# RMSNorm and a projection by 15 products: three transposes moved to TensorE, loads merged, the order laid out anew

## Chip, core and metric

The kernel runs on one core of a Trainium2 chip. The metric is the device time of one execution in microseconds. Engines: TensorE (PE; PEld is its weight load), VectorE (DVE), ScalarE (ACT), GpSimd (POOL), SyncE (SP), which here only issues DMA transfers, and 16 DMA engines behind its queue.

## The reference

```python
batch, n_heads, seq, head_dim = 8, 12, 1024, 64     # x is 8 x 1024 x 768, w_qkv is 768 x 2304
rms = np.sqrt(np.mean(x ** 2, axis=-1, keepdims=True) + eps)
x_norm = x / rms * gamma
return np.matmul(x_norm, w_qkv).astype(np.float32)
```

Inputs and output are float32. There are 8192 rows of x, 64 tiles of 128 rows; the output is 75.5 MB.

## The kernel before

**Two kinds of tiles.** The first seven tiles of x (the head, `N_HEAD`) are multiplied in the plain way. A tile is loaded (`load_x`), cast to bf16 (`cast`), turned by six 128x128 transposes on TensorE (`tr`, L509) and copied out of PSUM (`cp`); then six matmuls of 384 columns (`mm`, L520) give each of six column blocks, which are scaled by 1/rms on the way out of PSUM (`evac`) and stored (`store_h`). `stat` and `recip` give 1/rms: a square with a running sum on ScalarE, a root, a reciprocal. The weights come in twelve pieces of 576 KB (`load_w`) and are multiplied by gamma and cast to bf16 (`conv`). Gamma is turned from a row into columns by one transpose on TensorE (`gamma_tr`) and copied out by VectorE (`gamma_cp`). Fourteen matmuls on zeros (`idle`, L481) fill TensorE at the start.

**Triples.** The other 57 tiles are taken in 19 triples. Of a triple, three row blocks by two halves of K give six blocks of A; a half of the columns (1152) gives, by two halves of K and three column blocks, six blocks of B. The 18 block products of such a piece are computed as 15, of sums and differences of blocks. The sums of B are made once (`bound`, `scales`, `quad`, `bsum`, in f16 with one scale per half). For each triple:

- `load_t` (L580) loads a tile of x, one issue per tile, 384 KB; a triple's buffer `XI` is one of three.
- `pstat` (L583) squares it on ScalarE with a running sum, `prms` and `precip` give 1/rms for three tiles.
- `pcast` (L450 on ScalarE, L455 on VectorE) scales it to f16 into one of two buffers `XB`.
- `pxbar` (L602) turns the triple by one DMA transpose from SBUF to SBUF into one of three buffers `XT`. The functions `ptr` and `pcp`, six transposes on TensorE for a tile and a copy out of PSUM, are there and are not called by the order before.
- `osum` (L460) makes the eleven sums of A, mostly on GpSimd.
- `product` (L624) is three matmuls of 128x384. The 15 products of a triple and column half run in two chains (`CHAIN`), each in one PSUM bank, and add on to what the chain has; after each product the bank is read before the next product of the chain goes on.
- `hold` (L450 on ScalarE) reads a bank, scaled, into a part of the output the first time; `join` (L636, VectorE) reads it and adds or subtracts a part held before.
- `pstore` (L640) stores 128 rows by 1152 columns, 576 KB.

**What sets the order.** Everything is emitted in one order written out as text (`PLAN`): each item has a name, the engine and its arguments, and the loop at the end calls the function of that name. Each engine works through its own items in that order; between engines, waits are put in where data or buffers demand it. All transfers but gamma's go through SyncE's queue, in the order of the text: an item there that waits holds everything behind it.

Of the kernel before, what the change touches and what calls it, by code (L numbers as in the profile page):

```python
# [10 lines left out]
load_x SP 0 0;load_w SP 0 0 6;load_x SP 1;load_w SP 0 1 7;idle PE 14 512 0;load_x SP 2;load_w SP 0 2 8;load_w SP 0 3 9;  # L11
cast ACT 0 0;load_w SP 0 4 10;stat ACT 0;load_w SP 0 5 11;recip DVE 0;cast ACT 1;load_x SP 3 1;stat ACT 1;load_x SP 4;
tr PE 0 1;gamma_tr PE 2;recip DVE 1;cp ACT 0 0;tr PE 1 3;load_x SP 5;cast DVE 2;gamma_cp DVE;stat ACT 2;tr PE 2 4;cp DVE 1;
conv POOL 0 0 0 1;load_w SP 1 0 12;conv DVE 0 0 1 3;conv POOL 0 1 0 3;mm PE 0 0 0 5;mm PE 1 0 0 6;cp ACT 2;conv DVE 0 2 0 3;
mm PE 0 1 0 7;mm PE 1 1 0 1;mm PE 0 2 0 2;load_w SP 1 1 13;mm PE 1 2 0 3;mm PE 2 0 0 4;conv ACT 0 3 0 3;mm PE 0 0 1;
mm PE 1 0 1;mm PE 2 0 1;mm PE 0 1 1;load_w SP 1 2 6;mm PE 1 1 1;recip DVE 2;mm PE 0 2 1;bound ACT 0 0;bound DVE 0 1;
mm PE 1 2 1;conv POOL 0 4 0 3;mm PE 0 0 2;mm PE 1 0 2;mm PE 2 0 2;mm PE 0 1 2;mm PE 1 1 2;mm PE 0 2 2;load_w SP 1 3 7;
bound ACT 0 2;mm PE 1 2 2;mm PE 0 0 3;mm PE 1 0 3;conv DVE 0 5 0 3;mm PE 2 0 3;mm PE 0 1 3;mm PE 1 1 3;mm PE 0 2 3;
mm PE 1 2 3;bound ACT 0 3;bound DVE 0 4;mm PE 0 0 4;load_w SP 1 4 8;mm PE 1 0 4;mm PE 2 0 4;mm PE 0 1 4;mm PE 1 1 4;
mm PE 0 2 4;mm PE 1 2 4;mm PE 0 0 5;bound ACT 0 5;cast DVE 3 1;mm PE 1 0 5;mm PE 2 0 5;load_w SP 1 5 9;mm PE 0 1 5;  # L20
mm PE 1 1 5;evac DVE 0 0 10;mm PE 0 2 5;mm PE 1 2 5;evac ACT 1 0 11;cast DVE 4;mm PE 2 1 0 5;mm PE 2 1 1;mm PE 2 1 2;
load_x SP 6 2;evac ACT 0 1;fold DVE 0;mm PE 2 1 3;evac DVE 1 1;mm PE 2 1 4;bound_tr PE 0 6;conv POOL 1 0 0 3;mm PE 2 1 5;
evac ACT 0 2;tr PE 3 7;bound_top DVE 0;load_t SP 0 0 0;evac DVE 1 2;stat ACT 3;mm PE 2 2 0 1;mm PE 2 2 1;mm PE 2 2 2;
cp DVE 3 1;mm PE 2 2 3;conv POOL 1 1 0 3;mm PE 2 2 4;mm PE 2 2 5;tr PE 4 6;evac DVE 2 0 12;stat ACT 4;mm PE 3 0 0 2;
mm PE 3 0 1;recip DVE 3;mm PE 3 0 2;evac DVE 2 1;mm PE 3 0 3;conv POOL 1 2 0 3;mm PE 3 0 4;mm PE 3 0 5;evac DVE 2 2;cp ACT 4;
mm PE 3 1 0 3;mm PE 3 1 1;mm PE 3 1 2;mm PE 3 1 3;evac DVE 3 0 13;mm PE 3 1 4;mm PE 3 1 5;cast ACT 5;mm PE 3 2 0 7;
conv POOL 1 3 0 3;mm PE 3 2 1;recip DVE 4;mm PE 3 2 2;evac DVE 3 1;mm PE 3 2 3;store_h SP 0 0;mm PE 3 2 4;stat ACT 5;
mm PE 3 2 5;mm PE 4 0 0 4;bound DVE 1 0;mm PE 4 0 1;mm PE 4 0 2;mm PE 4 0 3;conv POOL 1 4 0 3;mm PE 4 0 4;mm PE 4 0 5;
evac ACT 3 2;bound_all PE 0 5;load_t SP 1 0 1;mm PE 4 1 0 1;evac DVE 4 0 6;mm PE 4 1 1;mm PE 4 1 2;bound ACT 1 1;mm PE 4 1 3;
tr PE 5 6;scales DVE 0;conv POOL 1 5 0 3;store_h SP 1 0;mm PE 4 1 4;recip DVE 5;mm PE 4 1 5;cp DVE 5;mm PE 4 2 0 2;  # L30
bound ACT 1 2;mm PE 4 2 1;mm PE 4 2 2;mm PE 4 2 3;evac DVE 4 1;quad POOL 0 0 0;mm PE 4 2 4;mm PE 4 2 5;store_h SP 2 0;
mm PE 5 0 0 3;mm PE 5 0 1;bound DVE 1 3;mm PE 5 0 2;load_t SP 0 1;pstat ACT 0 0;mm PE 5 0 3;mm PE 5 0 4;load_t SP 0 2;
mm PE 5 0 5;quad POOL 0 1 1;mm PE 5 1 0 7;mm PE 5 1 1;mm PE 5 1 2;evac ACT 4 2;mm PE 5 1 3;bound DVE 1 4;mm PE 5 1 4;
mm PE 5 1 5;bound ACT 1 5;mm PE 5 2 0 4;quad POOL 0 5 2;mm PE 5 2 1;mm PE 5 2 2;mm PE 5 2 3;mm PE 5 2 4;load_t SP 1 1;
mm PE 5 2 5;evac DVE 5 0 7;mm PE 0 3 0 5;mm PE 0 3 1;load_t SP 1 2;pstat ACT 1 0;mm PE 0 3 2;quad POOL 0 3 3;mm PE 0 3 3;
fold DVE 1;mm PE 0 3 4;evac DVE 5 1;mm PE 0 3 5;mm PE 1 3 0 6;mm PE 1 3 1;evac ACT 5 2;evac DVE 0 3 8;mm PE 1 3 2;
bound_tr PE 1 1;quad POOL 0 4 4;mm PE 1 3 3;quad ACT 0 2 5;mm PE 1 3 4;bsum DVE 0 15 add 0 1 6;mm PE 1 3 5;mm PE 2 3 0 2;
store_h SP 3 0;mm PE 2 3 1;mm PE 2 3 2;mm PE 2 3 3;mm PE 2 3 4;evac ACT 1 3 9;mm PE 2 3 5;mm PE 3 3 0 3;mm PE 3 3 1;
mm PE 3 3 2;evac ACT 2 3 10;bsum DVE 0 17 add 5 15 7;mm PE 3 3 3;store_h SP 4 0;mm PE 3 3 4;mm PE 3 3 5;pstat ACT 0 1;
mm PE 4 3 0 7;bound_top DVE 1;mm PE 4 3 1;mm PE 4 3 2;bsum DVE 0 14 sub 0 17 8;mm PE 4 3 3;mm PE 4 3 4;mm PE 4 3 5;  # L40
pstat ACT 0 2;mm PE 5 3 0 4;store_h SP 5 0;mm PE 5 3 1;evac DVE 3 3 11;mm PE 5 3 2;mm PE 5 3 3;mm PE 5 3 4;evac DVE 4 3 12;
mm PE 5 3 5;prms ACT 0;mm PE 0 4 0 5;mm PE 0 4 1;pstat ACT 1 1;mm PE 0 4 2;precip DVE 0;mm PE 0 4 3;bsum DVE 0 16 add 3 5 9;
mm PE 0 4 4;mm PE 0 4 5;mm PE 1 4 0 6;mm PE 1 4 1;pcast ACT 0 0 0;mm PE 1 4 2;bsum DVE 0 11 sub 14 3 10;mm PE 1 4 3;
mm PE 1 4 4;mm PE 1 4 5;mm PE 2 4 0 2;evac DVE 5 3 13;pstat ACT 1 2;mm PE 2 4 1;mm PE 2 4 2;mm PE 2 4 3;mm PE 2 4 4;
pcast DVE 0 1;mm PE 2 4 5;mm PE 3 4 0 1;pcast ACT 0 2;mm PE 3 4 1;mm PE 3 4 2;bsum DVE 0 7 add 4 5 11;mm PE 3 4 3;mm PE 3 4 4;
bound_all PE 1 3;mm PE 3 4 5;prms ACT 1;pxbar SP 0 0 3 2;bsum DVE 0 9 sub 5 2 12;mm PE 4 4 0 7;mm PE 4 4 1;evac ACT 0 4;
mm PE 4 4 2;mm PE 4 4 3;mm PE 4 4 4;precip DVE 1;evac ACT 1 4;mm PE 4 4 5;bsum DVE 0 10 add 3 7 13;mm PE 5 4 0 4;mm PE 5 4 1;
mm PE 5 4 2;pcast ACT 1 0 1;mm PE 5 4 3;bsum DVE 0 13 sub 9 17 14;mm PE 5 4 4;mm PE 5 4 5;mm PE 0 5 0 5;mm PE 0 5 1;
evac ACT 2 4;mm PE 0 5 2;pcast DVE 1 1;mm PE 0 5 3;mm PE 0 5 4;mm PE 0 5 5;pcast ACT 1 2;mm PE 1 5 0 6;load_t SP 2 0 0;
bsum DVE 0 6 sub 1 4 15;mm PE 1 5 1;mm PE 1 5 2;mm PE 1 5 3;mm PE 1 5 4;bsum DVE 0 8 add 1 2 16;evac ACT 3 4;mm PE 1 5 5;  # L50
mm PE 2 5 0 2;mm PE 2 5 1;mm PE 2 5 2;evac ACT 4 4;mm PE 2 5 3;bsum DVE 0 12 sub 17 10 17;mm PE 2 5 4;mm PE 2 5 5;
evac ACT 5 4;mm PE 3 5 0 1;pxbar SP 1 0 3 0;mm PE 3 5 1;osum DVE 0 6 add 1 5 0;mm PE 3 5 2;mm PE 3 5 3;evac ACT 0 5;
mm PE 3 5 4;osum DVE 0 11 sub 2 4 1;mm PE 3 5 5;mm PE 4 5 0 7;osum DVE 0 12 add 0 6 2;evac ACT 1 5;mm PE 4 5 1;mm PE 4 5 2;
osum DVE 0 13 sub 11 6 3;mm PE 4 5 3;mm PE 4 5 4;cast ACT 6 0;osum DVE 0 7 add 1 3 4;mm PE 4 5 5;product PE 0 0 10 4;
osum DVE 0 8 add 4 12 5;mm PE 5 5 0 5;osum DVE 0 9 add 7 13 6;evac ACT 2 5;product PE 0 0 2 6;osum DVE 0 15 add 0 1 7;
store_h SP 0 1;hold ACT 0 0 10 8 1 6;mm PE 5 5 1;osum DVE 0 14 add 2 3 8;tr PE 6 2;store_h SP 1 1;osum DVE 0 16 sub 4 14 9;
hold ACT 0 0 2 2 -1 7;product PE 0 0 3;store_h SP 2 1;osum DVE 0 10 add 0 2 10;evac ACT 3 5;mm PE 5 5 2;
bsum DVE 0 18 sub 13 11 18;product PE 0 0 12;evac ACT 4 5;mm PE 5 5 3;store_h SP 3 1;osum POOL 1 6 add 1 5 11;
osum DVE 1 11 sub 2 4 12;mm PE 5 5 4;mm PE 5 5 5;hold ACT 0 0 12 0 1;osum POOL 1 7 add 1 3 13;cp ACT 6 1;product PE 0 0 7;
osum DVE 1 12 add 0 6 14;store_h SP 4 1;hold ACT 0 0 3 4 -1 8;mm PE 6 0 0 1;mm PE 6 0 1;mm PE 6 0 2;  # L60
osum POOL 1 13 sub 11 6 15;stat ACT 6;mm PE 6 0 3;product PE 0 0 11;join DVE 0 0 7 6 -1 8 -1;mm PE 6 0 4;mm PE 6 0 5;
scales DVE 1;product PE 0 0 6;osum POOL 1 8 add 4 12 16;hold ACT 0 0 11 3 1;osum DVE 1 9 add 7 13 17;product PE 1 0 10 7;
hold ACT 0 0 6 7 1;product PE 0 0 13;osum POOL 1 15 add 0 1 18;hold ACT 1 0 10 8 1 9;osum DVE 1 14 add 2 3 19;
product PE 1 0 2 2;load_t SP 2 1;product PE 0 0 0;quad ACT 1 0 19;quad POOL 1 1 20;product PE 1 0 3;load_t SP 2 2;
join DVE 0 0 13 6 1 6 1;mm PE 6 1 0 3;mm PE 6 1 1;hold ACT 1 0 2 2 -1 10;mm PE 6 1 2;join DVE 0 0 0 1 -1 2 -1;
product PE 0 0 9;load_t SP 3 0 1;hold ACT 1 0 3 4 -1 11;quad POOL 1 5 21;osum DVE 1 16 sub 4 14 20;product PE 1 0 12;
join DVE 0 0 9 8 -1 8 1;evac ACT 5 5;product PE 0 0 1;bsum DVE 1 15 add 0 1 22;product PE 1 0 11;hold ACT 1 0 12 0 1;
# [305 lines left out]
def kernel(  # L373
# [199 lines left out]
    def rows(v, g, i):  # L573
        r0 = P * (N_HEAD + 3 * g + i)
        return v[r0:r0 + P, :]

    def load_t(eng, g, i, *slot):
        if slot:
            xi[g] = XI[slot[0]]
        nc.sync.dma_start(out=xi[g][:, i], in_=rows(xf, g, i))  # L580
# [104 lines left out]
```

## Time and profile before

| | |
|---|---|
| median of 3 runs | 361.82 us (358.01 to 362.8) |
| the profiled execution: time, span | 363.96 us, 362.2 us |
| mean granted clock | 0.987 |
| moved by DMA | 119.36 MB, 330 GB/s over the span |
| DMA issues, us to landing (median) | x: 64 of 384 KB, 6.5; stores: 82 + 46 of 576 KB, 5.5 and 5.6; weights: 12 of 576 KB, 10.0; transposes: 19, 7.1 |
| mean of one: hold, join, square, cast, sum of A | 579, 613, 840, 928, 923 ns |

The span is the time from the first to the last instruction. A line of a table of groups or waits names the engine, the tile and the line of the kernel; "SPq" is SyncE's queue. In the tables of windows a row has the stretch in us from the span's start, its length, then the busy time and the number of instructions of each engine, the granted TensorE clock as a share of full speed, the mean busy share of the 16 DMA engines (over 1 where packets overlap), and GB/s. In the table of waits a line has the total in us, the number of waits and the longest.

### The profile page before, as it was taken

How to read it: one execution, taken by the hardware profiler on the slowest of the kernel's cores; microseconds unless marked ns; L12 is line 12 of the kernel's file. 1: busy time of each engine (PE TensorE's matmuls, PEld its weight loads, DVE VectorE, ACT ScalarE, POOL GpSimd, SP SyncE). 2: the span in 40 equal slices, each digit the busy share in tenths (PEclk: the TensorE clock that was granted, in tenths of full speed). 3: DMA queues.
4: the chain of work that ended last, by engine and by line, in shares of the span. 5: the costliest groups of instructions: out<-in, count | busy, mean ns of one | idle time of the engine just before them, and what ended most of it. 6: DMA issues, size and time to landing. Idle time of an engine off the chain costs nothing.

```text
span 362.2 us, 6131 instructions
## 1 busy us (share of the span) xinstructions
PE 336.2 (93%) x2023; PEld 196.5 (54%) x2023; DVE 247.8 (68%) x456; ACT 259.4 (72%) x491; POOL 193.5 (53%) x218
## 2 busy tenths in 40 slices
PE   6799999998999799999999797999998989999993
PEld 2465556554654356556655464666565655656651
DVE  0799978897666467666866466676676666767764
ACT  5898989798975688568885665973987838854440
POOL 0359029008399735960938937099109974099100
PEclk9899999999999899999999999999999999999998
DMA  8999899999999999999999999999999999997466
GB/s 284 413 408 414 278 257 368 405 340 358 277 265 370 340 340 286 342 368 329 359 321 317 359 306 391 311 325 370 410 208 366 356 307 388 280 350 300 196 273 250
DMA packets 73804, 119.36 MB, mean 330 GB/s; under 512 B 47654, under 2 KB 47660, under 8 KB 73772
## 3 DMA queue, kind: packets, MB, share of 16 engines
q1 hardware_dynamic: 73760, 118.96, 99.2%
q8 instruction: 16, 0.26, 0.3%
q14 instruction: 16, 0.13, 0.1%
q10 hardware_dynamic: 12, 0.00, 0.0%
HBM read 32.25 MB, written 75.50 MB: 297 GB/s over the span
## 4 chain that ended last, share of the span: by engine, by line
PE 63%; DMA 18%; issue 5%; DVE 4%; ACT 4%; POOL 2%; SPq 2%; DVEq 0%; ACTq 0%; POOLq 0%
PE ps L624 52%; DMA xi<-in_x_dram 14%; PE ps L520 11%; DVE ot L636 3%; DMA xt<-xb 2%; POOL su L460 2%; ACT junk L583 2%; ACT ot L450 1%; DMA out_dram<-ot 1%; SPq L640 1%; DVE w_b L636 1%; PE ps L509 0%; DVE wh L460 0%; ACT w_b L450 0%; SPq L580 0%
## 5 line engine op out<-in xcount | busy, mean ns | idle before, releaser
L624 PE MATMUL ps<-wh,su 128*128 128x384 f16 x1254 | 229.8, 327 | 15.1 <-ACT ot L450 6.3
L624 PEld LDWEIGHTS <-su 128*128 128x128 f16 x1254 | 122.5, 98 | 101.5 <-issue 15.9
L460 POOL TENSOR_TENSOR su<-xt 128x384 f16<-128x384 f16 x106 | 96.2, 923 | 123.7 <-DMA xt<-xb 54.9
L636 DVE SCALAR_TENSOR_TENSOR ot<-ps,sc,ot 128x384 f32<-128x384 f32 x204 | 119.8, 613 | 53.7 <-PE ps L624 50.0
L636 DVE SCALAR_TENSOR_TENSOR w_b<-ps,sc,w_b 128x384 f32<-128x384 f32 x138 | 81.4, 613 | 36.0 <-PE ps L624 35.5
L450 ACT ACTIVATE ot<-ps,sc 128x384 f32<-128x384 f32 x136 | 75.6, 579 | 37.5 <-PE ps L624 36.3
L624 PE MATMUL ps<-wh,xt 128*128 128x384 f16 x456 | 95.8, 327 | 0.9 <-DVE ot L636 0.8
L583 ACT ACTIVATE junk<-xi 128x768 bf16<-128x768 f32 x57 | 47.9, 840 | 28.9 <-DMA xi<-in_x_dram 28.4
L450 ACT ACTIVATE w_b<-ps,sc 128x384 f32<-128x384 f32 x92 | 51.7, 578 | 19.7 <-PE ps L624 19.0
L624 PEld LDWEIGHTS <-xt 128*128 128x128 f16 x456 | 44.6, 98 | 31.5 <-issue 2.5
L450 ACT ACTIVATE xb<-xi,st 128x768 f16<-128x768 f32 x55 | 50.3, 928 | 0.8 <-DVE st L589 0.8
L460 POOL TENSOR_TENSOR su<-xt,su 128x384 f16<-128x384 f16 x52 | 47.6, 915 | 1.3
L520 PE MATMUL ps<-w_b,xt 128*128 128x384 bf16 x252 | 46.6, 334 | 0.3 <-POOL w_b L457 0.2
L520 PEld LDWEIGHTS <-xt 128*128 128x128 bf16 x252 | 24.7, 100 | 17.3 <-issue 1.9
L460 POOL TENSOR_TENSOR su<-su,su 128x384 f16<-128x384 f16 x35 | 32.2, 919 | 0.0
L457 POOL TENSOR_SCALAR w_b<-ot,g_sb 128x1152 bf16<-128x1152 f32 (+1 forms) x9 | 10.7, 1190 | 17.2 <-DVE g_sb L488 9.3
L460 DVE TENSOR_TENSOR wh<-wh,wh 128x1152 f16<-128x1152 f16 x26 | 19.7, 788 | 0.1
L450 ACT ACTIVATE ot<-ps,rs 128x384 f32<-128x384 f32 x26 | 13.6, 575 | 0.0
L457 POOL TENSOR_SCALAR wh<-w_b,sc 128x1152 f16<-128x1152 bf16 x9 | 11.6, 1308 | 0.0
L583 ACT ACTIVATION_READ_ACCUMULATOR junk<-xi 128x1 f32 x57 | 10.9, 191 | 0.0
L455 DVE TENSOR_SCALAR ot<-ps,rs 128x384 f32<-128x384 f32 x16 | 9.5, 607 | 0.9 <-DMA out_dram<-ot 0.6
L542 ACT ACTIVATE junk<-w_b 128x1152 bf16<-128x1152 bf16 x7 | 8.1, 1157 | 0.7 <-DVE w_b L455 0.6
(47 smaller groups left out, 73.8 us busy)
## 6 DMA issues: line engine op xcount, KB each, us to landing
out_dram<-ot SPq DMA_DIRECT2D x82, 576.0 KB, 5.5
out_dram<-w_b SPq DMA_DIRECT2D x46, 576.0 KB, 5.6
xi<-in_x_dram SPq DMA_DIRECT2D x64, 384.0 KB, 6.5
ot<-in_w_qkv_dram SPq DMA_DIRECT2D x12, 576.0 KB, 10.0
xt<-xb SPq DMA_TRANSPOSE x19, 7.1
g<-in_gamma_dram ACTq DMA_DIRECT2D x1, 3.0 KB
```

What stands on the lines that cost most here:

```text
L450: nc.scalar.activation(out=out, in_=in_, func=AF.Copy, scale=scale, bias=0.0)
L455: nc.vector.tensor_scalar(out=out, in0=in_, scalar1=scale, scalar2=None, op0=mult)
L457: nc.gpsimd.tensor_scalar(out=out, in0=in_, scalar1=scale, scalar2=1.0, op0=mult, op1=mult)
L460: (nc.vector if eng == "DVE" else nc.gpsimd).tensor_tensor(out=out, in0=in0, in1=in1, op=op)
L520: nc.tensor.matmul(out=po["p", t, w], lhsT=head_xt(t)[:, k, :], rhs=w_b[:, k // H, w, k % H], start=(k == 0), stop=(k == KO - 1))
L542: nc.scalar.activation(out=junk, in_=v, func=AF.Abs, accum_out=o)
L583: nc.scalar.activation(out=junk[:, :K], in_=xi[g][:, i], func=AF.Square, accum_out=ST[g % 6][:, i:i + 1])
L624: nc.tensor.matmul(out=o, lhsT=a[:, k, :], rhs=b[:, k, :], start=(r in FIRST and k == 0), stop=(k == H - 1), skip_group_check=True)
L636: nc.vector.scalar_tensor_tensor(out=part(g, c, i, slot), in0=po[g, c, CHAIN[r]], scalar=(sc if sign > 0 else nsc)[c], in1=part(g, c, j), ...
L640: nc.sync.dma_start(out=rows(of, g, i)[:, HW * c:HW * (c + 1)], in_=ot[g, c, i])
```

## The change

Three functions change, and the text of the order is a new one. `load_t` now loads the three tiles of a triple by one transfer (1152 KB); `rows` goes, and `pstore` spells its address out, with the same effect.

```diff
-    def load_t(eng, g, i, *slot):
-        if slot:
-            xi[g] = XI[slot[0]]
-        nc.sync.dma_start(out=xi[g][:, i], in_=rows(xf, g, i))
+    def load_t(eng, g, slot):
+        xi[g] = XI[slot]
+        r0 = P * (N_HEAD + 3 * g)
+        nc.sync.dma_start(out=xi[g], in_=xf[r0:r0 + 3 * P, :].rearrange("(i p) k -> p i k", p=P))
```

In the order, triples 2, 8 and 14 are turned by nine `ptr` and nine `pcp` (seven on ScalarE, two on VectorE) and no `pxbar`:

```diff
+product PE 13 0 0;join DVE 13 0 9 8 -1 8 1;ptr PE 14 0 0;join DVE 13 0 0 1 -1 2 -1;product PE 13 0 5;pcp ACT 14 0 1;
+ptr PE 14 2 4;join DVE 13 0 5 5 -1 4 -1;product PE 13 0 1;osum POOL 14 15 add 0 1 24;load_t SP 17 0;pcp ACT 14 2 1;
```

The start, with gamma's transpose ahead of the fourteen matmuls on zeros, and the first copies `cp` behind the casts and squares of three tiles (the removed lines are the first three of the order before):

```diff
-load_x SP 0 0;load_w SP 0 0 6;load_x SP 1;load_w SP 0 1 7;idle PE 14 512 0;load_x SP 2;load_w SP 0 2 8;load_w SP 0 3 9;
-cast ACT 0 0;load_w SP 0 4 10;stat ACT 0;load_w SP 0 5 11;recip DVE 0;cast ACT 1;load_x SP 3 1;stat ACT 1;load_x SP 4;
-tr PE 0 1;gamma_tr PE 2;recip DVE 1;cp ACT 0 0;tr PE 1 3;load_x SP 5;cast DVE 2;gamma_cp DVE;stat ACT 2;tr PE 2 4;cp DVE 1;
+load_x SP 0 0;load_w SP 0 0 6;load_x SP 1;load_w SP 0 1 7;load_x SP 2;load_w SP 0 2 8;load_w SP 0 3 9;cast ACT 0 0;
+load_w SP 0 4 10;gamma_tr PE 0;load_w SP 0 5 11;idle PE 14 512 1;stat ACT 0;load_x SP 3 1;gamma_cp DVE;load_x SP 4;
+conv POOL 0 0 0 1;conv DVE 0 0 1 3;load_x SP 5;recip DVE 0;load_w SP 1 0 12;cast ACT 1;stat ACT 1;load_w SP 1 1 13;
+conv DVE 0 1 0 3;recip DVE 1;cast ACT 2;load_w SP 1 2 6;stat ACT 2;tr PE 0 2;tr PE 1 3;conv DVE 0 2 0 3;load_w SP 1 3 7;
+tr PE 2 4;cp ACT 0 0;recip DVE 2;bound DVE 0 0;conv POOL 0 3 0 3;bound ACT 0 1;mm PE 0 0 0 5;mm PE 0 1 0 6;load_w SP 1 4 8;
```

The count of items, where it differs:

| item | before | after |
|---|---|---|
| `load_t` | 57 | 19 |
| `pxbar` | 19 | 16 |
| `ptr` (TensorE), `pcp` (ScalarE, VectorE) | 0, 0 | 9, 7 + 2 |
| `hold` on ScalarE, on VectorE | 228, 0 | 167, 61 |
| `osum` on GpSimd, on VectorE | 193, 16 | 198, 11 |
| `evac` on ScalarE, on VectorE | 26, 16 | 23, 19 |
| `pcast` on ScalarE, on VectorE | 55, 2 | 57, 0 |

The matmuls of the head and the products stay as many (252 and 1710). In the new order a `pxbar` mostly stands just behind the last product of the triple that used its `XT` buffer before, the next `load_t` behind it and six `pstore` after that; before, the three `load_t` of a triple lay scattered among the stores. Of one such place, SyncE's items and some of the others:

```
product PE 3 1 14; product PE 4 0 0; pxbar SP 6 0 3 2; ...; load_t SP 8 0; ...; pstore SP 3 1 0; ...;
hold ACT 4 1 6 7 1; pstat ACT 8 0; hold ACT 5 0 11 3 1; pstat ACT 8 1; pstat ACT 8 2; ...
```

## Prediction

> **What bounds the kernel now.** I read the page first, then the windows of 10 us, SyncE's queue in order of time, the table of waits and the chain.
>
> ```profile
> PE 336.2 (93%) x2023; PEld 196.5 (54%) x2023; DVE 247.8 (68%) x456; ACT 259.4 (72%) x491; POOL 193.5 (53%) x218
> ...
> q1 hardware_dynamic: 73760, 118.96, 99.2%
> ...
> PE 63%; DMA 18%; issue 5%; DVE 4%; ACT 4%; POOL 2%; SPq 2%; DVEq 0%; ACTq 0%; POOLq 0%
> ```
>
> Two resources look full at once: TensorE at 93%, and the DMA queue, whose packets take 99.2% of 16 engines' span. The windows (time; PE, PEld, DVE, ACT, POOL busy; clock, DMA share, GB/s) tell where:
>
> ```profile
> 20.00:30.00 10.00, 10.00 (x75) 6.13 (x73) 8.93 (x22) 8.86 (x19) 8.02 (x7) 1.00 1.02 409
> ...
> 110.00:120.00 10.00, 6.81 (x40) 3.71 (x39) 5.60 (x10) 5.36 (x11) 7.87 (x9) 1.00 1.09 339
> 120.00:130.00 10.00, 9.88 (x51) 5.51 (x51) 5.13 (x10) 5.82 (x12) 9.43 (x11) 0.83 1.01 379
> ...
> 260.00:270.00 10.00, 10.00 (x64) 6.04 (x62) 7.19 (x15) 9.03 (x18) 0.00 (x0) 1.00 1.13 260
> ...
> 340.00:350.00 10.00, 10.00 (x63) 6.00 (x62) 6.92 (x13) 4.74 (x9) 0.00 (x0) 1.00 0.59 236
> ```
>
> With plain loads the DMA moves 409 to 414 GB/s (10 to 40 us). Wherever a transpose lies, the share is as high and the rate is 260 to 340. SyncE's queue around one, and the DMA's share in slices of 0.25 us from 262 to 272 us:
>
> ```profile
> 261.86 5.51 SPq L602 DMA_TRANSPOSE xt<-xb  x1
> 267.47 0.53 SPq L640 DMA_DIRECT2D out_dram<-ot  x1
> 268.05 0.42 SPq L580 DMA_DIRECT2D xi<-in_x_dram  x1
> ...
> 319.50 3.20 SPq L602 DMA_TRANSPOSE xt<-xb  x1
> ```
> ```profile
> DMA  8999894999760000100399999997997999597699
> ```
>
> While SyncE issues a transpose (5.0 us at the median of 19) nothing behind it is issued, the queue runs dry (the zeros, near 265 to 267 us), and only then do the transpose's packets flow. I priced this from the order of the queue. Take 384 KB (0.393 MB) a tile of x, 576 KB (0.590 MB) a weight load or store, 0.412 MB per us, a start of 2 us, and c for each transpose ahead. Ahead of the last transpose stand 64 tiles of x, 12 weight loads, 111 stores (97.7 MB) and 18 transposes: 2 + 237.1 + 18c = 319.5, c = 4.5 us. Ahead of triple 9's, issued at 179.31: 56.8 MB and 9, c = 4.4; of triple 13's, at 238.02: 73.9 MB and 13, c = 4.4. With 4.4 us this **DMA line** meets all 19 issue times within 2 us. TensorE's line doesn't: work ahead of the last transpose is 289.5 us (252 + 3 x 501 matmuls at 0.1636, from 20.65 us for 126 in the chain, plus 42 transposes); with the first matmul at 11.4 and 1.7 us lost to a half clock from 11.8 to 15.2 us it would be there at 302.6, and is there at 319.5. So 16.9 us of stalls up to there; the largest, at 110 to 120 us, also brought a half clock (0.83 in the window after). From 330 us on the DMA has room and TensorE is full. The stalls reach TensorE through ScalarE, which takes its instructions in order and stands at a square (L583) until x lands, with evictions behind it:
>
> ```profile
> ACT junk L583 <- DMA xi<-in_x_dram: 28.4, 17, 3.3
> ...
> PE ps L624 <- ACT ot L450: 6.3, 8, 2.4
> ...
> PE ps L624 <- POOL su L460: 4.4, 7, 1.0
> ...
> PE ps L624 <- ACT w_b L450: 3.5, 2, 2.3
> ```
>
> **The change, part by part.**
>
> *Three DMA transposes go (triples 2, 8, 14).* 3 x 4.4 = 13.2 us off the DMA line. Ahead of the last transpose now stand 95.9 MB and 15 of them: 2 + 232.8 + 66 = 300.9, against 318.4. The Trainium skill speaks against this gain: its page "Advanced Engine Details and Errata", section "X-Bar Transpose (TRN2)", says such DMAs are as fast as regular ones, at 350 to 400 GB/s. By that, my estimate for 0.59 MB would be 1.5 to 1.7 us each, some 5 us in all; the zeros in the strip above don't agree, and the trace decides.
>
> *TensorE takes them over.* 9 x 6 transposes. The chain has the head's:
>
> ```profile
> 22.58 0.34 PE ps L509 x6
> ```
>
> 9 x 0.34 = 3.1 us, all on TensorE's path. Their input was bf16, here it is f16; I take the same, bounded by the trace's 0.22 us of a lone transpose (54 x 0.22 = 12 us if none overlapped) and 0. The page "TensorE: Matmul & The Clock Gate", section "Part 4: PE-mode transpose", gives about 275 ns for one in a kernel; that would be 14.9 us by my estimate and would eat the gain, but the row of six in 0.34 us contradicts it. The nine copies out of PSUM cost ScalarE 7 x 0.78 and VectorE 2 x 0.55 us, beside matmuls.
>
> *One load for three tiles.* 57 issues become 19; 38 x 0.91 us (the median of L580) come off SyncE's queue, which waits more than it works, so I count nothing. But the first tile is there only with the third: 2 x 0.393 / 0.412 = 1.9 us later. In the new order the load stands right behind a transpose, mostly, and that transpose directly behind the last product of the triple three before, whose buffer it takes: it cannot go earlier. In the written order, counted in TensorE's work, 8.8 us lie from such a transpose to the first square of the load behind it (triple 6's transpose at 108.5, triple 8's first square at 117.3; there are ten such places, from 7.9 to 9.3). On the chip: 5.0 for the issue, 0.1, then the landing. The first transfer behind a transpose, a store of 0.59 MB, landed after 3.0 to 5.3 us, 3.5 at the median; 1.18 MB is 1.4 more, so 10.0 us in sum (9.5 to 11.8). The square is 1.2 us late. Behind it on ScalarE stand the other two squares and holds (L450), which read a PSUM bank before TensorE may add into it again. Of 28.4 us that ScalarE lost before, 9.8 (a third) appear as waits of TensorE for it; all of it is the other end. Between them I take 0.6: 0.7 us in each of ten places, 7 us.
>
> The same sum from the DMA side: between two transposes with six stores and a load lie 4.4 + 4.72 / 0.412 = 15.8 us of DMA against 14.7 to 15.7 of TensorE; taking the longer of the two in each interval from triple 3 to 18 gives 220.5 against 213.5, 7 us. The two are one effect seen twice, not to be added. I take 7.
>
> *61 holds to VectorE, five sums to GpSimd.* VectorE: 61 x 0.607 = +37, less 5 x 0.45, so 248 becomes about 284 us, 79%; ScalarE 259 - 35 + 5.5 = 230, 64%. Per triple VectorE gets 18 joins at 0.613 and some 3 holds, 13 us of 15. Below the bound, nothing. One place is worse: in TensorE's work from 60 to 75 us (end of the head, triple 2's transposes and casts) ScalarE has 18.8 us by the rows' means, 17.3 before; I add 2 us, from 0 to 4.
>
> *The start.* Gamma's turn goes ahead of the 14 warm-up matmuls, so they wait for its load (there by 6.2 us at the latest, where before's turn found it; over by 11.4 at the latest, 5.2 us later). The first copy out of PSUM now stands on ScalarE behind the cast and square of tile 2, which lands at 10.0: 10.0 + 0.83 + 0.84 + 0.19 + 0.29 + 0.78 = 12.9, first matmul at 13.0, not 11.4: +1.6 (0 to 3). The half clock may stay or go (0 or -1.7); I keep it.
>
> *The end* keeps its form: 5.2 us from the last matmul, 357.0, to 362.2, and 3.6 us of stalls after the last transpose.
>
> **Sum.** 362.2 + 3.1 + 1.6 + (7 + 2 - 16.9 = -7.9) = 359.0 us of span. The profiled execution took 363.96, 1.8 over its span; so 360.8, and scaled to the median shown (361.82 / 363.96) 358.7. I say **358.5**, a gain near 1%: most of what the DMA gives back goes into transposes, a later start and late loads.
>
> **Rivals.**
>
> - *The lines meet smoothly.* TensorE's line reaches the last transpose at 284.7 + 13.0 + 1.7 = 299.4, the DMA's at 300.9. Left then are 41.8 us of work, 3.6 and 5.2: 351.5, as a median 351. For it: casts end 12 to 15 us ahead of their transposes, and products start some 20 us behind them, so that late transposes are covered. Against it: no interval has DMA time to spare.
> - *The late load decides (slower).* Place: ScalarE at the first square behind a transpose. If the load lands 12 us after the transpose's issue (an issue of 6.5, as the 6.45 at 190.32, or a landing of 6.9), the square is 3.2 late, and with 0.6 of it on TensorE in ten places that is 19 us of stalls: 362.2 + 4.7 + 2 + 19 - 16.9 = 371, as a median 369 to 370; all passed on, 13 more. It loses against before from a landing 10.5 us after the issue, by over 2% from 11.7.
> - *The transposes weren't the price.* The DMA line fits because SyncE's stores wait on VectorE (L640 waits 84 us for joins), and TensorE's stalls come from the order of ScalarE. Then all 16.9 stay, and 362.2 + 4.7 = 366.9, as a median 366.5.
>
> **Chances.** Forecast 0.46, smooth 0.27, late load 0.17, transposes not the price 0.10. 2% is about what a measurement of this kernel can tell from no change (358.0 to 362.8 in three runs); the bounds are 354.6 and 369.1. Faster: the smooth case and the edge of the forecast, 0.29; slower: the late load, whose full end is far out, and the edge of the last case, 0.18; within 2%: 0.53. The range takes in the smooth case and the lower part of the late load: 350.5 to 370.
>
> **What would show it.** Right: 16 DMA transposes, the last issued near 308 us, not 319.5; squares waiting for x about once per triple, 1 to 2 us; transposes of six in 0.34 us; the first product matmul near 13.0. Smooth: last transpose by 302, ScalarE's waits for x under 15 us. Late load: over 35 us of such waits and TensorE waiting on L450 over 15. I am wrong if six transposes take over 0.6 us, if VectorE is what TensorE waits for, or if the last transpose still comes after 315.

## The result

The kernel became **slower**: 379.8 us (median of four runs, 375.86 to 381.3) against 362.1 of the kernel before on the same chip, a ratio of 1.051 with a 95% interval of 1.045 to 1.0575. The prediction, 358.5 us in 350.5 to 370, was wrong. The rival with the late load named the right side and the right place, at too small a price. All ratios here and below compare fast runs alone; a run more than 1.5% above the fastest of its kernel is left out of them.

The profiled execution of the changed kernel took 380.52 us with a span of 378.6 us and a mean granted clock of 0.976 (before: 0.987). Lines of its page, those that answer to the page of before: the busy time of each engine, the queue's share, the shares of the chain that ended last, and the issues of x and of the transposes (number, KB, median us to landing).

```profile
PE 343.1 (91%) x2077; PEld 201.5 (53%) x2077; DVE 282.5 (75%) x516; ACT 236.8 (63%) x435; POOL 198.3 (52%) x222
...
q1 hardware_dynamic: 66144, 117.19, 93.5%
...
PE 42%; DMA 35%; SPq 6%; DVE 5%; ACT 4%; POOL 4%; issue 3%; DVEq 0%; ACTq 0%
...
xi<-in_x_dram SPq DMA_DIRECT2D x19, 1152.0 KB, 7.3
...
xt<-xb SPq DMA_TRANSPOSE x16, 6.4
```

The DMA queue is less full than before (93.5% against 99.2%), but the chain runs through the DMA for 35% of the span, where it was 18%. The table of waits tells where: ScalarE at the square, and TensorE on ScalarE's reading of PSUM banks (L445 is the line that was L450). The waits of TensorE on ScalarE there were 9.8 us before and are 20.2 now.

```profile
ACT junk L574 <- DMA xi<-in_x_dram: 39.2, 15, 5.2
...
PE ps L615 <- ACT ot L445: 13.3, 9, 2.9
...
PE ps L615 <- ACT w_b L445: 6.9, 6, 3.1
```

One place of the ten that the prediction spoke of, triple 6's transpose and triple 8's load. First SyncE's queue, then ScalarE, then TensorE, each in order of time; a line has start, duration, engine, line, operation and count, and in brackets the idle time before it with its releaser.

```profile
131.75 4.75 SPq L593 DMA_TRANSPOSE xt<-xb  x1
136.55 0.57 SPq L571 DMA_DIRECT2D xi<-in_x_dram  x1
137.22 1.37 SPq L632 DMA_DIRECT2D out_dram<-w_b  x2
```
```profile
139.03 1.56 ACT L445 ACTIVATE ot<-ps,sc 128x384 f32<-128x384 f32 x3 [1.86 <-PE ps L615]
143.56 0.84 ACT L574 ACTIVATE junk<-xi 128x768 bf16<-128x768 f32 x1 [2.97 <-DMA xi<-in_x_dram]
144.31 0.19 ACT L574 ACTIVATION_READ_ACCUMULATOR junk<-xi 128x1 f32 x1
144.40 0.56 ACT L445 ACTIVATE ot<-ps,sc 128x384 f32<-128x384 f32 x1
```
```profile
142.73 0.65 PE L615 MATMUL ps<-wh,su 128*128 128x384 f16 x3
145.01 1.14 PE L615 MATMUL ps<-wh,su 128*128 128x384 f16 x6 [1.64 <-ACT ot L445]
```

The load is issued at 136.55 and its last byte is there at 143.5: 7.0 us after its issue, 11.8 after the transpose's. ScalarE stands at the square from 140.6, because the instruction is the next in its order, and the hold (144.40) that would free the bank for TensorE stands behind it. At the next place the transpose is issued at 148.81, the load at 153.73, the square starts at 161.08 (12.3 after the transpose's issue) after 4.41 us of idle time, and TensorE goes on at 163.50 after 3.06 us. In all ten places with a transpose just ahead the load landed 10.0 to 14.0 us after the transpose's issue, 11.5 at the median, and 5.9 to 7.9 us after its own, 7.1 at the median.

That stall costs more than its length. The lines of the next place, and the windows (time; PE, PEld, DVE, ACT, POOL busy; clock, DMA share, GB/s), show it:

```profile
161.08 0.84 ACT L574 ACTIVATE junk<-xi 128x768 bf16<-128x768 f32 x1 [4.41 <-DMA xi<-in_x_dram]
163.50 1.12 PE L615 MATMUL ps<-wh,su 128*128 128x384 f16 x3 [3.06 <-ACT w_b L445]
164.42 4.05 PE L615 MATMUL ps<-wh,xt 128*128 128x384 f16 x12
```
```profile
150.00:160.00 10.00, 10.00 (x64) 6.01 (x62) 8.09 (x16) 5.28 (x8) 4.43 (x6) 1.00 0.99 226
160.00:170.00 10.00, 6.93 (x26) 3.32 (x25) 4.41 (x8) 4.04 (x9) 5.19 (x6) 0.66 0.95 386
```

From 160 to 170 us TensorE did 26 matmuls, not 64: it stood, and then ran with a granted clock of 0.66 in the mean. The twelve matmuls at 164.42 take 4.05 us, twice the 0.1636 us each of full speed. After the first 20 us, windows with 0.83 or less lie at 110, 160 and 260 us; in their shares of 10 us, twice the missing clock is 3.4 + 6.8 + 3.4 us at half speed, so some 6.8 us of time. Before had one such window in the middle (0.83 at 120 to 130). Both have one at 10 to 20 us besides.

Why 7.0 us to land? The DMA's rate in slices of 0.25 us from 136 to 146 us:

```profile
GB/s 9 260 291 289 291 290 290 241 61 98 160 135 135 197 307 283 270 307 393 307 184 111 233 295 393 449 418 442 436 424 424 406 406 442 406 461 406 424 387 424
```

Until 138.0 the transpose's packets flow, at 290 GB/s. From there to 143.5 the 22 slices sum to 1.5 MB. The packets in the trace can be told apart by their size (3072 bytes for x, 4608 for a store): 1.15 MB of it are the load's, and of the stores only 0.01 MB starts before 142.5, when the load is nearly through. So the stores behind don't hold the load up. Its own packets flow slowly: 61 to 197 GB/s in the first 1.5 us, and 1.18 MB in 5.3 us, 221 GB/s, where the prediction took 412. In the ten places with a transpose just ahead the load's rate is 206 to 278 GB/s. What makes it slow there is not shown.

### The profile page after: what moved, and what is told of

The parts are those of the page before. It is cut to its first block, busy times and chain, and to the rows that moved or that the text cites. A ratio compares the mean times of both kernels' runs of the same rounds, so it can differ in the third digit from the quotient of the medians.

```text
span 378.6 us, 6138 instructions
## 1 busy us (share of the span) xinstructions
PE 343.1 (91%) x2077; PEld 201.5 (53%) x2077; DVE 282.5 (75%) x516; ACT 236.8 (63%) x435; POOL 198.3 (52%) x222
## 3 DMA queue, kind: packets, MB, share of 16 engines
q1 hardware_dynamic: 66144, 117.19, 93.5%
## 4 chain that ended last, share of the span: by engine, by line
PE 42%; DMA 35%; SPq 6%; DVE 5%; ACT 4%; POOL 4%; issue 3%; DVEq 0%; ACTq 0%
PE ps L615 40%; DMA xi<-in_x_dram 21%; DMA out_dram<-ot 6%; DMA out_dram<-w_b 4%; SPq L593 4%; POOL su L455 4%; DVE ot L627 3%; DMA ot<-in_w_qkv_dram 3%; ACT junk L574 2%; PE ps L515 2%; DMA xt<-xb 2%; ACT ot L445 1%; SPq L468 1%; ACT w_b L445 1%; DVE bnd L535 1%
## 5 line engine op out<-in xcount | busy, mean ns | idle before, releaser
L455 POOL TENSOR_TENSOR su<-xt 128x384 f16<-128x384 f16 x108 | 98.9, 932 | 113.1 <-ACT xt L443 38.5
L627 DVE SCALAR_TENSOR_TENSOR w_b<-ps,sc,w_b 128x384 f32<-128x384 f32 x141 | 83.4, 612 | 23.1 <-PE ps L615 21.0
L445 ACT ACTIVATE ot<-ps,sc 128x384 f32<-128x384 f32 x101 | 57.4, 579 | 57.0 <-PE ps L615 54.8
L574 ACT ACTIVATE junk<-xi 128x768 bf16<-128x768 f32 x57 | 48.0, 843 | 39.8 <-DMA xi<-in_x_dram 39.2
L445 ACT ACTIVATE w_b<-ps,sc 128x384 f32<-128x384 f32 x66 | 37.5, 579 | 24.5 <-PE ps L615 24.2
L445 ACT ACTIVATE xb<-xi,st 128x768 f16<-128x768 f32 x57 | 50.4, 928 | 0.1
L455 POOL TENSOR_TENSOR su<-xt,su 128x384 f16<-128x384 f16 x54 | 50.0, 927 | 0.6
L450 DVE TENSOR_SCALAR ot<-ps,sc 128x384 f32<-128x384 f32 x33 | 20.1, 612 | 4.6 <-PE ps L615 2.8
L455 DVE TENSOR_TENSOR wh<-wh,wh 128x1152 f16<-128x1152 f16 x26 | 21.8, 864 | 0.0
L450 DVE TENSOR_SCALAR w_b<-ps,sc 128x384 f32<-128x384 f32 x28 | 17.1, 612 | 3.4 <-PE ps L615 3.2
L452 POOL TENSOR_SCALAR wh<-w_b,sc 128x1152 f16<-128x1152 bf16 x8 | 10.6, 1343 | 14.5 <-DVE sc L556 14.5
L450 DVE TENSOR_SCALAR ot<-ps,rs 128x384 f32<-128x384 f32 x19 | 11.2, 608 | 2.8 <-PE ps L515 2.8
L445 ACT ACTIVATE ot<-ps,rs 128x384 f32<-128x384 f32 x23 | 12.3, 576 | 1.0 <-issue 1.0
```

The source lines that it names most:

```text
L445: nc.scalar.activation(out=out, in_=in_, func=AF.Copy, scale=scale, bias=0.0)
L450: nc.vector.tensor_scalar(out=out, in0=in_, scalar1=scale, scalar2=None, op0=mult)
L452: nc.gpsimd.tensor_scalar(out=out, in0=in_, scalar1=scale, scalar2=1.0, op0=mult, op1=mult)
L455: (nc.vector if eng == "DVE" else nc.gpsimd).tensor_tensor(out=out, in0=in0, in1=in1, op=op)
L574: nc.scalar.activation(out=junk[:, :K], in_=xi[g][:, i], func=AF.Square, accum_out=ST[g % 6][:, i:i + 1])
L627: nc.vector.scalar_tensor_tensor(out=part(g, c, i, slot), in0=po[g, c, CHAIN[r]], scalar=(sc if sign > 0 else nsc)[c], in1=part(g, c, j), ...
```

## The experiments

Three theories were to be told apart. **Late load**: ScalarE waits for all 1.18 MB where single loads would give it the first tile early. **Transposes**: DMA or TensorE transposes, or their new places, cost the time. **Order**: the new order, with 61 holds on VectorE and the squares elsewhere, costs it. Medians of "before" in these sessions lie between 361.5 and 363.3 us; ratios are to those, with 95% intervals.

**Three loads again.** The only edit to the changed kernel, at the same places in the order:

```diff
-        nc.sync.dma_start(out=xi[g], in_=xf[r0:r0 + 3 * P, :].rearrange("(i p) k -> p i k", p=P))
+        for i in range(3):
+            nc.sync.dma_start(out=xi[g][:, i], in_=xf[r0 + P * i:r0 + P * (i + 1), :])
```

> The changed kernel with each merged load cut into three, one per tile, issued one behind the other in the same place. If the size of the load counts, the first tile lands 1 to 2 us sooner, the squares wait 20 to 28 us in sum and the time is 364 to 373. If only its place behind the transpose counts, the time stays at 377 to 381.

Measured: 359.45 us, ratio 0.995 (0.988 to 1.0016). The whole loss is gone, some 20 us, with the same transposes, holds and order. Waits of this kernel, then SyncE and ScalarE around one place:

```profile
ACT junk L599 <- DMA xi<-in_x_dram: 21.6, 20, 3.5
...
PE ps L640 <- ACT ot L469: 5.8, 7, 1.3
...
PE ps L640 <- ACT w_b L469: 1.8, 1, 1.8
```
```profile
203.29 5.67 SPq L618 DMA_TRANSPOSE xt<-xb  x1
209.00 1.52 SPq L596 DMA_DIRECT2D xi<-in_x_dram  x3
```
```profile
212.67 0.84 ACT L599 ACTIVATE junk<-xi 128x768 bf16<-128x768 f32 x1 [1.52 <-DMA xi<-in_x_dram]
...
214.41 0.84 ACT L599 ACTIVATE junk<-xi 128x768 bf16<-128x768 f32 x1 [0.80 <-DMA xi<-in_x_dram]
...
215.93 0.84 ACT L599 ACTIVATE junk<-xi 128x768 bf16<-128x768 f32 x1 [0.58 <-DMA xi<-in_x_dram]
```

The three issues take 1.52 us of SyncE's time instead of 0.57. The first tile is there 3.7 us after the load's issue, the third 6.9 us after it: about when the one load of three landed. In the ten places the first tile lands 3.5 to 5.1 us after the issue and the third 6.0 to 7.4. So the transfer was hardly slowed by being one; what was lost is the first tile, 3.3 us earlier here, and with it that the wait comes in three short pieces.

The span differs by 378.6 - 357.8 = 20.8 us. TensorE's idle time holds 13.4 of it (35.5 against 22.1), nearly all of that its waits on ScalarE (20.2 against 7.6). Its busy time holds the other 7.4 (343.1 against 335.7 for the same matmuls), of which the half clock explains some 6.8. ScalarE's waits at the square fell by 17.6 us. This split is that of one execution. Another execution of the changed kernel had a mean clock of 0.992, as high as with three loads, and still took 375.86 us, 16 us more than three loads: the loss does not need the half clock.

**The squares don't wait.** The merged load is kept, but the squares of a triple read the triple before. This kernel leaves out the right 1/rms: each triple's is taken from other rows.

```diff
-        nc.scalar.activation(out=junk[:, :K], in_=xi[g][:, i], func=AF.Square, accum_out=ST[g % 6][:, i:i + 1])
+        nc.scalar.activation(out=junk[:, :K], in_=xi[max(g - 1, 0)][:, i], func=AF.Square, accum_out=ST[g % 6][:, i:i + 1])
```

> The changed kernel with the squares of a triple taken from the triple before, whose x has long landed (1/rms is then that of other rows; all instructions and transfers stay). If ScalarE standing at the first square is the cause, the waits for x vanish there, a few may show at the casts, and the time is 350 to 358, the case in which DMA and TensorE meet smoothly. If the stalls come from elsewhere, it stays at 372 or more.

Measured: 361.12 us, ratio 0.997 (0.994 to 1.001), clock 0.992. The load lands as late as ever, and nobody minds; the squares wait 2.2 us in sum:

```profile
xi<-in_x_dram SPq DMA_DIRECT2D x19, 1152.0 KB, 7.3
```
```profile
ACT junk L598 <- DMA xi<-in_x_dram: 2.2, 2, 1.7
...
PE ps L639 <- POOL su L479: 4.5, 1, 4.5
```

So with the load at this place neither its bytes nor its lateness in the queue make the loss: it is the wait at the square. The 350 to 358 that I hoped for was too low; one wait of 4.5 us of TensorE for a sum stays, among others.

**Only the merged load, in the kernel before.** The three loads of a triple become one, at the place of the first; order, transposes and holds of before stay.

```diff
-load_t SP 8 0 0;pxbar SP 6 0 3 2;pstore SP 4 0 1;pstore SP 4 1 2;pstore SP 4 0 0;load_t SP 8 1;
+load_t SP 8 0;pxbar SP 6 0 3 2;pstore SP 4 0 1;pstore SP 4 1 2;pstore SP 4 0 0;
```

> The kernel before with one change: the three loads of a triple by one transfer, at the place of the first. If a merged load costs where the first square follows closely (3 to 9 us of TensorE's work there), ScalarE's waits for x grow from 28 us to 40 or more and the time is 367 to 376. If the loss in the changed kernel came only from the place behind a transpose, 359 to 364.

Measured: 382.17 us, ratio 1.056 (1.046 to 1.065), clock 0.966. Alone it costs what the whole change costs. Here the load comes ahead of the transpose, and it is late in another way too: the transposes behind it are held up. Waits of this kernel:

```profile
POOL su L477 <- DMA xt<-xb: 107.9, 11, 21.8
...
ACT junk L600 <- DMA xi<-in_x_dram: 32.2, 9, 6.1
...
PE ps L641 <- ACT ot L467: 12.4, 8, 4.7
...
PE ps L641 <- POOL su L477: 7.7, 6, 4.3
```

GpSimd waited 54.9 us for transposes in the kernel before, in fewer and shorter waits; here it is 107.9. TensorE's waits for GpSimd's sums go from 4.4 to 7.7 us, those for ScalarE from 9.8 to 15.8. The expectation was missed on both sides: the squares wait 32.2 us, not 40 or more, and the time is above 376. Of the 18.4 us by which the span grew, 10.1 are TensorE's idle time and 8.3 its busy time for the same matmuls; four spells at half clock after the first 20 us, 20.4 us together, answer to the latter.

**Only the TensorE transposes, in the kernel before.** Triples 2, 8 and 14 by `ptr` and `pcp`, three loads per triple, holds where they were.

> The kernel before with one change: triples 2, 8 and 14 are turned by TensorE, copies on ScalarE and VectorE, and their three DMA transposes go; loads, holds and all else stay. By the DMA line 13 us less there and 3 to 5 us more on TensorE's path: 352 to 357. If the transposes on the DMA were not the price, 363 to 367.

Measured: 357.42 us, ratio 0.990 (0.987 to 0.9935). A gain of 1%, clear of zero, just above the 352 to 357 that were expected: the last transpose's issue moves from 319.50 to 315.01, not by 13 us as the DMA line has it.

```profile
315.01 2.79 SPq L626 DMA_TRANSPOSE xt<-xb  x1
```

TensorE's idle time goes from 26.0 to 21.1 us. The gain is 3.5 us (0.97% of 361.5). If the 3.1 us of TensorE's own transposes are all on the path, a DMA transpose was worth 2.2 us here (1.8 to 2.6): half of the DMA line's 4.4, in the kernel that the line was fitted to.

**The merged load ahead of the transpose.** Twelve loads of the changed kernel trade places with the transpose in front of them.

```diff
-pstore SP 3 1 1;pxbar SP 6 0 3 2;load_t SP 8 0;pstore SP 3 1 0;
+pstore SP 3 1 1;load_t SP 8 0;pxbar SP 6 0 3 2;pstore SP 3 1 0;
```

> The changed kernel with twelve of its nineteen merged loads (triples 2, 3, 6 to 9, 11 to 15, 17) moved from behind a DMA transpose to just ahead of it. Late load: the first square no longer waits for an issue of 5 us plus a landing of 7; ScalarE's waits for x at the squares fall from 39 us to under 15, TensorE's waits for ScalarE from 20 to under 8, and the time from 379.8 to 355 to 364. If the new order itself or VectorE's 61 holds are the cause, it stays at 374 or more. If the transposes' lateness is passed on in place of the loads', GpSimd is what TensorE waits for and the time stays above 368.

Measured: 372.47 us, ratio 1.030 (1.023 to 1.038). None of the three cases holds whole. The time is that of the third (above 368), but TensorE waited more for ScalarE (10.5 us) than for sums of A (4.2 us, GpSimd's and VectorE's). The squares still wait 26.2 us in 13 places, for now the load lands 9.3 us after its issue (7.3 behind the transpose), and the transposes land after 9.9, not 6.4.

**The merged load four places earlier** in SyncE's queue.

```diff
-pstore SP 3 0 1;pstore SP 3 0 2;pstore SP 3 1 2;pstore SP 3 1 1;pxbar SP 6 0 3 2;load_t SP 8 0;
+pstore SP 3 0 1;load_t SP 8 0;pstore SP 3 0 2;pstore SP 3 1 2;pstore SP 3 1 1;pxbar SP 6 0 3 2;
```

> The changed kernel, loads merged, each load of triples 2 to 18 moved four places up in SyncE's queue (never ahead of the last cast of the triple that had its buffer), so that three or four stores lie between it and the next transpose. If lateness at the first square is the cause, a merged load does no harm there: squares wait under 12 us in sum, TensorE under 6 for ScalarE, 353 to 361. If a merged load harms by what it does to the queue (transposes and stores behind 1.2 MB), 368 or more, as with the load just ahead of the transpose (372).

Measured: 371.56 us, ratio 1.027 (1.019 to 1.036). The squares wait only 8.3 us, and TensorE for ScalarE 1.8; as far as that goes the cure works. But the transposes now land after 12.0 us at the median, and one of them ends in the longest stall of all these kernels. The two lines for that, then SyncE, ScalarE and TensorE there:

```profile
ACT junk L597 <- DMA xi<-in_x_dram: 8.3, 6, 2.6
...
xt<-xb SPq DMA_TRANSPOSE x16, 12.0
```
```profile
176.92 11.31 SPq L616 DMA_TRANSPOSE xt<-xb  x1
```
```profile
190.64 0.93 ACT L468 ACTIVATE xb<-xi,st 128x768 f16<-128x768 f32 x1 [9.01 <-DMA xt<-xb]
```
```profile
195.04 1.14 PE L638 MATMUL ps<-wh,su 128*128 128x384 f16 x3 [8.28 <-POOL su L478]
```

The transpose's issue took 11.31 us, a cast waited 9 us for it to free its buffer `XB`, and the sum of A that needs a later tile made TensorE wait 8.28 us. The mean clock was 0.967. A transfer of 1.18 MB ahead of a transpose delays the transpose; behind it, it is late itself. What lengthens the issue can be read from the traces: it lasts until everything ahead of it in the queue has landed. Ahead of this one six transfers were under way, the load among them, and the last of them landed 11.3 us after the issue began. In the 14 kernels here, 176 DMA transposes had transfers ahead that landed more than 3 us after the transpose's issue began; the issue ended 0.2 us after the last landing at the median, and between 0.2 us before it and 1.7 us after it in all of them.

**Three loads, the first tile's ahead of the transpose**, the two others behind it.

> The changed kernel with three loads per triple; the first tile's load stands just ahead of the DMA transpose (where there is one by), the other two behind it. 0.4 MB ahead should delay the transpose by 1 us only. If the rest of the waits at squares is what keeps three loads in place (359.5) from going lower, squares wait under 14 us (from 21.6) and the time is 352 to 358. If the transposes pass their delay on, as with the merged load ahead (372), 361 to 368.

Measured: 359.21 us, ratio 0.996 (0.992 to 0.9996), between the two ranges and no better than all three behind it, though the squares wait 17.5 us instead of 21.6. The rest of that wait is not what holds this kernel.

**Triples 8 and 14 by DMA again**, first with the merged load, then with three loads.

```diff
-product PE 13 0 0;join DVE 13 0 9 8 -1 8 1;ptr PE 14 0 0;join DVE 13 0 0 1 -1 2 -1;
+product PE 13 0 0;join DVE 13 0 9 8 -1 8 1;join DVE 13 0 0 1 -1 2 -1;
```

> The changed kernel with triples 8 and 14 turned by DMA again, each transpose issued behind the last product that used its buffer, as the others are; triple 2 stays on TensorE. If each transpose ahead of a load costs a stall of 2 to 3 us, two more of them, less 2 us of TensorE's transposes and copies, give 381 to 386. If transposes on the DMA cost nothing on the path, 376 to 379.

> Three loads per triple in the place of the merged one (359.5), and triples 8 and 14 turned by DMA again. With merged loads this cost 9 us. If the DMA line binds, two transposes more cost 2 x 4.4 less 2 us on TensorE, 363 to 367. If the cost of a transpose was only the late load behind it, 358 to 361.

Measured: 389.08 us, ratio 1.074 (1.068 to 1.080), with the merged load, above both of its ranges, and 366.39, ratio 1.013 (1.003 to 1.023), without. Against the same kernels with TensorE's transposes that is some 8 us more (1.074 - 1.051 of 362) and 6.5 us more (1.013 - 0.995). Two DMA transposes cost that net of the 2 x 1.0 us that TensorE spares, so some 4.3 us each with three loads. That is near the 4.4 of the DMA line, but the intervals of the two ratios leave it open by about 2 us either way. With the merged load each further transpose is one more place for a late square: 50.1 us at the squares, from 39.2.

**The 61 holds back on ScalarE**, three loads.

> Three loads per triple in the place of the merged one, and the 61 holds of VectorE back on ScalarE. If ScalarE standing at a square is what delays holds, holds on VectorE are free of it, and taking them back costs 3 to 9 us: 362 to 368. If VectorE at 79% busy was itself a drag, 354 to 358.

Measured: 366.65 us, ratio 1.014 (1.004 to 1.023), some 7 us more than with the holds on VectorE. The intervals leave some 4 us either way. Of the waits of TensorE, those on ScalarE went from 7.6 to 10.6 us. So the move pays, though not by the way the expectation has it: the squares wait less here, 11.4 us against 21.6. What the holds gain on VectorE was not traced further.

**Five and six triples turned by TensorE**, three loads. Triples 5 and 11, then 17 as well, get `ptr` and `pcp` like the other three.

> Three loads per triple in the merged load's place, and triples 5 and 11 turned by TensorE too, so five of nineteen. Two fewer DMA transposes gave 5 to 7 us between 18 and 16 of them; if the DMA still binds, 2 x (4.4 less 1.0 to 2) more: 353 to 357. If TensorE's order binds by now, 359 to 363.

> As with five triples turned by TensorE (354.3), and triple 17 too, six of nineteen, three loads per triple. Triple 17's transpose lies where the DMA has room already (share 0.9 from 320 us on), so 1 us more on TensorE against at most 2 gained: 353 to 356. If the DMA still bound there, 350 to 352.

Measured: 354.28 us, ratio 0.982 (0.975 to 0.989), and 354.95, ratio 0.980 (0.9755 to 0.985), each against before in its own session. **Both beat both kernels**; the sixth adds nothing that can be measured. Between three triples and five lie 4.7 us (0.995 - 0.982 of 362); with the 2 x 1.0 us that TensorE takes over, a DMA transpose is 3.4 us here, again open by about 2 us. With five, TensorE is busy for 337.1 of 353.2 us, and its waits on ScalarE in the triples are down to 1.3 us. The waits at the square:

```profile
ACT junk L601 <- DMA xi<-in_x_dram: 10.0, 11, 2.1
```

## Why the prediction was wrong

The sum was 362.2 + 3.1 + 1.6 + (7 + 2 - 16.9) = 359.0 us of span; measured 378.6, 19.6 more. Two terms carry the miss.

**The late load: 7 us said, 20.8 measured** (against three loads at the same places). The mechanism was the one described: a load behind a transpose, ScalarE at the square, holds behind it, TensorE. Three sizes in it were off:

- *The landing.* "3.5 at the median; 1.18 MB is 1.4 more", 4.9 us, was taken from stores of 0.59 MB, with the load's further bytes at the queue's 412 GB/s. The load landed 5.9 to 7.9 us after its issue, 7.1 at the median: about 1.3 us until the transpose's packets are through, then its own at 206 to 278 GB/s. The issue of the transpose was shorter than the 5.0 taken (3.9 at the median), so from the transpose's issue to the load's landing it is 11.5 us at the median of the ten places (10.0 to 14.0), not 10.0. The prediction's range for that was 9.5 to 11.8, and four of the ten places lie above it; it also named 11.7 as the point from which the change loses over 2%.
- *The places.* Ten times 1.2 us, 12 us in sum, were expected at the squares. Measured: 39.2 us in 15 waits, 17.6 more than with three loads.
- *The half clock.* Of the 17.6 us, 12.6 reached TensorE as waits, 0.7 of it, not far from the 0.6 taken. But 7.4 us more came in the profiled execution as busy time for the same matmuls, nearly all of it a lower granted clock, and no term stood for that, although the prediction saw it in the profile of before: "the largest, at 110 to 120 us, also brought a half clock". In the 14 profiles there are 20 spells at half clock between the first 20 us and the last matmul, each of 3.4, 6.8 or 10.2 us, and every one begins during a wait of TensorE of 2.2 to 8.3 us or at most 1.3 us after it. The 12 waits of 3.1 us and more all have one; of the 14 from 2.2 to 3.0 us eight have one. That the waits bring the spells about is argued from this; no run changed the clock alone.

**The stalls given back: 16.9 us said.** Without the late load the sum is 352.0 us of span; the kernel with three loads has 357.8, so about 5.8 of the 16.9 did not come back (the rest of the sum, as the items below have it, was off by little; the 2 us for ScalarE in it were not measured alone). What failed is the DMA line as a floor that TensorE stands on. For its price of 4.4 us a transpose the runs give three figures: 4.3 from the two that were put back and 3.4 from the two more that were taken away, each open by about 2 us, and 2.2 (1.8 to 2.6) from the three in the kernel before. Nor does it tell when TensorE goes on: with 16 transposes it put the last one at 300.9 us, and three loads have it at 308.82; with 14, where the line falls by another 8.8, it is 304.09. For the kernel before with three triples turned it gives 305 (318.4 less 13.2), and it is 315.01.

```profile
308.82 3.06 SPq L618 DMA_TRANSPOSE xt<-xb  x1
```

A fit that holds for 19 issue times of one kernel said how that kernel went, where TensorE and the queue wait for each other; it was not the cause of all its stalls. What the stalls that stayed came from is open, and so is what gave the others back: part of it may be the holds' move to VectorE, since undoing that costs 7 us. The two misses, 13.8 and 5.8, make up the 19.6 by the way they are counted.

The other terms, with the lines for the first of them:

```profile
81.28 0.83 PE L598 MATMUL ps<-ident_h,xb 128*128 128x128 f16 x12
81.95 0.65 PE L615 MATMUL ps<-wh,xt 128*128 128x384 f16 x3
```

- *TensorE's transposes, 3.1 us*: right. Twelve at 81.28 us take 0.67 us to the next matmul, 0.34 for six. The Trainium skill's 275 ns for one transpose ("TensorE: Matmul & The Clock Gate", section "Part 4: PE-mode transpose") does not hold for transposes in a row here: 219 ns is the duration of one, 56 ns what it adds.
- *DMA transposes as the price*: right in sign, and its rival (they cost nothing) falls: putting two back costs 6.5 us, taking two more away gives 4.7. The skill's page "Advanced Engine Details and Errata", section "X-Bar Transpose (TRN2)", has such a transfer as fast as a regular one, my estimate from it being 1.5 to 1.7 us for 0.59 MB; the prices measured here, 2.2 us (1.8 to 2.6) in the comparison with the narrowest interval, lie above that.
- *The start, +1.6*: +1.2. Gamma is there by 2.23 us, the first matmul of the head at 12.56.
- *VectorE, nothing*: right in the busy time (282.5 us, said 284). But the move was worth some 7 us with three loads, as the run with the holds put back shows, and the prediction counted nothing for it.
- *The end*: as said; 5.3 us from the last matmul to the end of the span.

Of the rivals, **the late load** was right in its place and in the number that decides ("if the load lands 12 us after the transpose's issue"). It gave 369 to 370 (its own sum of 371 makes 370.6), or 13 more if all is passed on; measured 379.8, near the far end. That it ended there is in part chance: it had no term for the clock either. It had 0.17, because the estimate of the landing lay below its threshold, and that estimate came from a store of half the load's size, scaled at a rate that the load did not have. **Smooth** asked for a last transpose by 302 us and never came, though the version with five triples turned gets within 3.5 us of its time.

By its own signs ("over 35 us of such waits and TensorE waiting on L450 over 15") the profile answers to the late load: 39.2 and 20.2 us. "If the last transpose still comes after 315" it is wrong: 329.69.

## What to carry to other kernels

A transfer's consumer waits for its last byte. Before loads are merged to save issues, look who takes the first piece, what stands behind that consumer on its engine, and how long the queue is when the transfer starts; here three issues in place of one took SyncE 1 us more a triple, and the kernel was 20 us faster. Moving the large load earlier does not mend it where something else in the queue is as urgent.

Price a landing from a transfer of the same kind and size in the same surroundings, and give it the rate of those surroundings, not the queue's mean. Look what a DMA transpose has ahead of it in its queue: here its issue ended when the last of that had landed. And where the profile shows a stall followed by a lower clock, count the clock with the stall.

## What was not expected of the hardware

- A DMA transpose's issue holds SyncE for 2.4 to 12.3 us. Where transfers ahead of it took more than 3 us to land, it lasted until the last of them had landed: 4.75 us behind stores, 11.31 with 1.18 MB of load among the six transfers still under way. Its data landed some 2 us after that (6.60 us after the issue began in the first case, 13.36 in the second).
- A load just behind a DMA transpose moved its 1.18 MB at 206 to 278 GB/s, where loads and stores together moved 409 to 414 at the start of the kernel before. The stores issued 0.7 us and more behind it did not cause that: in the place shown 0.01 MB of theirs had started when the load was nearly through.
- Three loads of 0.39 MB, one after the other, bring the first tile 3.7 us and the third 6.9 us after the issue of the first; one load of 1.18 MB brings all of it after 7.0. Each extra issue took about half a microsecond of SyncE's time.
- Spells of 3.4 us and more at half clock stood at waits of TensorE from 2.2 us on: 20 spells in 14 profiles, and none elsewhere between the first 20 us and the last matmul.
